# Accumulating the second third of Down's weight sums behind chunk 4's gated parts, with norm 2's vectors and one form tile moved

## The chip, the cores and the metric

The kernel runs on one core of one Trainium2 chip. The metric is device time in microseconds from the start of the program to its end; the profile describes one execution in detail, and the timed runs give the median.

## What is computed

One decoder layer on 256 tokens of width 1024: a causal pooling mixer and block attention side by side, a cross-attention into 256 memory tokens, and a gated feed-forward part of width 2816, each followed by a residual and a layer norm. The change lies in the last part.

```python
def swiglu(h, w_gate, w_up, w_down):
    return (jax.nn.silu(h @ w_gate) * (h @ w_up)) @ w_down

# per layer
h = layer_norm(ALPHA * h + mix, ln1_g, ln1_b)
h = layer_norm(ALPHA * h + memory_cross_attention(h, mem, w_xq, w_xkv, w_xo), ln2_g, ln2_b)
h = layer_norm(ALPHA * h + swiglu(h, w_gate, w_up, w_down), ln3_g, ln3_b)
```

## The kernel before

**Numbers in two parts.** Every matrix product is made from values split into a high part (rounded, by ACT, line 159 for weights) and a low part (the remainder, by DVE, line 175), with three matmuls in place of one. So each 512 KB block of weights passes through SP's load (line 107; line 104 for blocks that hold one quarter), ACT's cast and DVE's subtraction before PE can use it. `Stream` does this in order; there are seven raw places for loads, and a load is issued when DVE's subtraction has freed one. The blocks have numbers: w65 to w68 are chunk 0 of gate and up, four more for each chunk, w85 to w98 the row chunks, w99 to w102 chunk 7, w103 to w106 chunk 8, and so on.

**Feed-forward, first half.** Gate and up are computed in chunks of 256 columns, `for c in range(1, NFC)`. Chunks 5 and 6 (`ROWS`) are computed together by `Rows`, a seven-product scheme for 2 x 2 blocks that needs sums and differences of the activations (`make_forms`, in the tiles `extra0` and `extra1`) and of the weights. Every other chunk is a `Gated`: PE fills four PSUM banks (lines 482 and 488), `add` has ACT copy and DVE add their halves (lines 1331 and 1332), `multiply` applies silu and the product, and `split` makes the forms of the result and its two parts (lines 717 to 719, 534 and 535). The results of chunk c are added at the end of its turn, and multiplied and split within the turn of the next. Odd chunks use the banks of one PSUM pool, even ones those of the other, so a chunk waits for the `add` of the chunk two before; the row products start with the odd pool and come to banks of chunk 4 with their sixth product. Their own sums leave their banks through `Rows.leave` (lines 1424 to 1439), beginning with an ACT copy on line 1424; chunk 7 needs those banks.

**Feed-forward, second half.** Down uses the same seven-product scheme for nine of eleven chunks (`SUMMED`) and needs sums of weight quarters. DMA makes them in DRAM, in thirds: SP copies quarters from `w_sum` to `sum_z` and `sum_w` (`begin_sums`, line 424, and `begin_second`, line 428, tied to the loads of chunks 1, 2 and 8), and POOL adds to them with accumulating transfers (`add_quarters`, line 435): first a double quarter into `sum_z`, then, when that has landed, one of its halves into `sum_w`:

```python
def add_quarters(i):
    js = slice(i * THIRD, (i + 1) * THIRD)
    add_to(sum_z[:, :, js], w_sum[:, 2:4, js])
    add_to(sum_w[:, js], sum_z[:, 1, js])
```

The second third is read by the loads of Down's chunks 4 to 6, from w128 on.

**Order.** The schedule is written out by hand: each engine runs its instructions in the order in which the program text issues them, and `run(gu, n)` advances PE's generator by n steps between other work. POOL has little to do but these transfers and a few small norm operations, and a transfer that waits holds up all behind it on POOL.

**Norm 2.** The rows of token tile 0 are first brought to mean 0 and variance 1, which suffices for the feed-forward input; `vectors` later applies gain and bias in four DVE operations (lines 939 and 941, two each), for the residual of norm 3. They free the tile `gb2` with gain and bias.

**Places.** Tiles of 8 KB a partition share eleven places in the pool `ap` and one in the pool `late`; a new tile takes a free place. The place in `late` holds weights of chunk 0 (w67) and, from chunk 8 on, the gated parts of chunk 8.

Of the kernel before, what the change touches and what calls it, by code (L numbers as in the profile page):

```python
# [8 lines left out]
F32 = mybir.dt.float32  # L9
F32R = mybir.dt.float32r  # L10
# [4 lines left out]
P = 128  # L15
D = 1024
S = 256
T = S // P
KD = D // P
# [24 lines left out]
ROWS = (5, 6)  # L44
# [5 lines left out]
def r32(t):  # L50
    return t.bitcast(F32)


class Stream:
# [136 lines left out]
    def next(self):  # L191

        if not self.held:
            self.prepare(min(self.used + self.ahead, len(self.tiles) + 1))
# [27 lines left out]
def decoder_layer(  # L222
# [3 lines left out]
    nc = tc.nc  # L226
# [4 lines left out]
    ap = ctx.enter_context(tc.tile_pool(name="acts", bufs=A8_BUFS))  # L231
    sp = ctx.enter_context(tc.tile_pool(name="small", bufs=3))
# [6 lines left out]
    def a8(name, dt=F32):  # L239
        return ap.tile([P, KD, S], dt, tag="a8", name=name)  # L240
# [193 lines left out]
    def add_to(dst, src):  # L434
        nc.gpsimd.dma_start(dst, src, accum_op=OP.add, max_dma_last_dim=8192)  # L435
# [5 lines that stand above are left out]
# [33 lines left out]
    def proj_both(pss, numbers, yT, group=KD):  # L474

        for k0 in range(0, KD, group):
            for k in range(k0, k0 + group):
                hi, _ = ws.get(numbers, k)  # L480
                for b, ps in enumerate(pss):
                    nc.tensor.matmul(ps, hi[:, b * P:(b + 1) * P], yT.both(k), start=k == 0, stop=False,  # L482
                                     skip_group_check=True)
                yield
            for k in range(k0, k0 + group):
                _, lo = ws.parts_of(numbers, k)
                for b, ps in enumerate(pss):
                    nc.tensor.matmul(ps[:, S:], lo[:, b * P:(b + 1) * P], yT.pair(k)[0], start=False,  # L488
                                     stop=k == KD - 1, skip_group_check=True)
                ws.done(numbers, k)  # L490
                if ws.pace == 1:
                    ws.next()
                yield
# [31 lines left out]
    def run(gen, n=None):  # L525

        while n is None or n > 0:
            if next(gen, gen) is gen:
                return False
            n = None if n is None else n - 1  # L530
        return True
# [339 lines left out]
    late = ctx.enter_context(tc.tile_pool(name="late", bufs=LATE_BUFS))  # L871
# [410 lines left out]
    gT, shared = {}, []  # L1282
# [26 lines left out]
    def gated_t():  # L1309
        pt = bank("pgt").rearrange("p (f t) -> p f t", f=2)  # L1310
        for t in range(T):
            for f in range(2):
                nc.tensor.transpose(pt[:, f, t * P:(t + 1) * P], sg0[:, t, f * P:(f + 1) * P], ident)
        gated_parts(0)
        split(gT[0][0], gT[0][1], pt.rearrange("p f (t s) -> p (f t) s", t=T))
# [32 lines left out]
    def make_forms():  # L1348

        q = h2f.rearrange("p (j f) (t s) -> p j f t s", f=2, t=2)  # L1350
        at = {(f, t): q[:, :, f, t] for f in range(2) for t in range(2)}
        nc.vector.tensor_sub(at[1, 1], at[0, 1], at[1, 1])
        yield
        nc.vector.tensor_sub(at[0, 1], at[0, 0], at[0, 1])
        yield
        nc.vector.tensor_sub(at[0, 0], at[1, 1], at[0, 0])
        yield
        nc.vector.tensor_add(at[1, 0], at[1, 0], at[0, 0])
        yield
        for j in (0, 4):  # L1360
            hi, lo = (y[:, j:j + 4] for y in extra)
            nc.scalar.copy(hi, h2f[:, j:j + 4])
            yield
            nc.vector.tensor_sub(lo, h2f[:, j:j + 4], r32(hi))
            yield
# [109 lines left out]
    run(proj_n({1: first[1]}, c_gu[0], h2T))  # L1475
    gated_row(1, first[1])
    left, rows, later = None, None, norms[0].vectors()
    extra = [a8(f"extra{i}", F32R) for i in range(2)]
    more_forms = make_forms()
    for c in range(1, NFC):  # L1480
        if c == ROWS[0]:
            run(more_forms)
            rows = Rows()
            gu = rows.products()
            run(gu, 3)
            left.multiply()
            run(gu, 3)
            left.split()
            run(gu, 16)
            ws.held = True  # L1490
            run(gu)
            ws.held = False
            left = rows
        if c in ROWS:
            continue
        pss = [(accbank if c % 2 else bank)("pg") for _ in range(4)]
        if c == 3:
            ws.ahead += 1
            ws.widen("spare", sp)
            for i in range(2):  # L1500
                add_quarters(i)
        if c == 7:
            add_quarters(2)
        gu = proj_both(pss, c_gu[c], h2T, KD if c < NFC - 3 else 4)
        run(gu, 2)
        if left:
            left.multiply()
        run(gu, 2)
        if c < ROWS[0]:
            run(more_forms, 2)  # L1510
        if left and left is rows:
            run(gu, 3)
            left.transposed()
            left.split()
        elif left:
            left.split()
            run(later, 2)
        else:
            run(gu, 4)
            gated_t()  # L1520
        if c >= 2:
            run(gu, 7)
            ws.held = True
        run(gu)
        left = Gated(c, pss)
        left.add()
        ws.held = False
# [174 lines left out]
```

## Time and profile before

| what | value |
|---|---|
| median of 3 runs | 397.82 us (397.03 to 397.84) |
| profiled execution | 393.9 us |
| its span, first to last instruction | 391.6 us |
| PE busy | 367.2 us, 94% |
| DVE busy | 342.3 us, 87% |
| ACT busy | 231.8 us, 59% |
| POOL busy | 36.4 us, 9% |
| hardware DMA queue q1 | 93.41 MB, 64.7% of 16 engines |
| software DMA queue q0 | 13.37 MB, 17.2% of 16 engines |

All times in the rows below count from the start of the span. A timeline row is one instruction, or several alike in sequence, with the idle time of its engine before it and what ended that, in brackets. q0 carries the transfers that POOL issues, q1 those of SP. PE's busy time is modelled, so its idle times say more than its busy share.

### The profile page before, as it was taken

The page shows a single profiled execution, that of the slowest core. Times are in us where ns is not written, and L with a number is a line of the kernel's source. Part 1 is how long each engine was busy: PE and PEld are TensorE (multiplying, and loading weights), DVE is VectorE, ACT ScalarE, POOL GpSimd, SP SyncE. Part 2 cuts the span into 40 slices and gives each one's busy share as a digit, 9 for nine tenths or more (in the row PEclk, how much of TensorE's full clock was granted, in tenths as well). Part 3 has the DMA queues.
Part 4 walks back from the last instruction along what each step waited for, and adds up shares of the span by engine and source line. Part 5 has one row for each costly group of instructions (what it writes and reads, how often), then busy time and mean ns, then how long its engine had stood idle before and what let it go on. Part 6 is the DMA issues. An engine that isn't in the chain of part 4 may idle for free.

```text
span 391.6 us, 5502 instructions
## 1 busy us (share of the span) xinstructions
PE 367.2 (94%) x1941; PEld 311.7 (80%) x1941; DVE 342.3 (87%) x523; ACT 231.8 (59%) x356; POOL 36.4 (9%) x41
## 2 busy tenths in 40 slices
PE   9999999999999999999999999296489999999994
PEld 8888878888888899888888888284269888888882
DVE  6889899999999999899695889886767889899995
ACT  5768766774544756764474556565437756677702
POOL 0000047300310010000210000001000000000003
PEclk9999999999999999999999999689599999999999
DMA  7999996879869999999999984469997456889602
GB/s 262 412 412 362 258 402 199 330 231 338 233 142 324 386 368 261 354 315 413 270 294 256 343 271 166 154 215 347 304 344 257 157 180 200 284 284 318 230 0 107
DMA packets 33754, 107.58 MB, mean 275 GB/s; under 512 B 3264, under 2 KB 4544, under 8 KB 32320
## 3 DMA queue, kind: packets, MB, share of 16 engines
q1 hardware_dynamic: 31056, 93.41, 64.7%
q0 software_dynamic: 2240, 13.37, 17.2%
q10 hardware_dynamic: 432, 0.46, 0.3%
q8 instruction: 15, 0.25, 0.2%
q14 instruction: 11, 0.09, 0.1%
HBM read 106.18 MB, written 27.79 MB: 342 GB/s over the span
## 4 chain that ended last, share of the span: by engine, by line
PE 72%; DVE 13%; DMA 7%; issue 4%; ACT 3%; DVEq 0%; ACTq 0%
PE pg L482 11%; PE pg L488 6%; DMA w107r<-in_w_gu 5%; PE pxq L482 4%; PE pxk L482 4%; PE pqk L601 4%; PE m L467 3%; PE m L469 3%; PE m L468 3%; PE x L467 2%; PE x L469 2%; PE x L468 2%; PE pqk L604 2%; PE pxk L488 2%; PE pxq L488 2%
## 5 line engine op out<-in xcount | busy, mean ns | idle before, releaser
L534 ACT CAST g<-sq 128x1024 fp32r<-128x1024 f32 x9 | 9.4, 1050 | 25.6 <-DVE sq L719 25.6
L535 DVE TENSOR_TENSOR g<-sq,g 128x1024 fp32r<-128x1024 f32 x9 | 11.0, 1226 | 10.2 <-ACT g L534 10.2
L906 POOL TENSOR_TENSOR rs<-mv,mhalf 128x1 f32<-128x1 f32 x6 | 4.3, 723 | 146.4 <-DVE mv L904 146.4
L482 PE MATMUL pg<-h2T,w99h 128*128 128x512 f32 x8 | 4.7, 711 | 9.0 <-ACT row L1424 8.5
L666 ACT ACTIVATE pr<-pr,mx 128x128 f32<-128x128 f32 (+1 forms) x16 | 7.1, 445 | 7.7 <-DVE mx L697 7.7
L482 PEld LDWEIGHTS pg<-h2T,w99h 128*128 128x128 f32 x8 | 2.4, 309 | 11.1 <-ACT row L1424 8.9
L895 DVE BATCH_NORM_STATS2 st<-r 128x6 f32<-128x512 f32 (+1 forms) x12 | 8.1, 672 | 0.4
L435 POOL DMA_DIRECT2D sum_z<-in_w_sum x3 | 3.5, 1155 | 51.2 <-DMA sum_z<-in_w_sum 51.2
L467 PE MATMUL g<-w85h,extra 128*128 128x512 f32 x1 | 0.8, 794 | 7.4 <-DVE sq L1332 7.4
L560 ACT ACTIVATE h2f<-tp,turned 128x128 f32<-128x128 f32 x8 | 3.0, 455 | 7.0 <-PE tp L557 7.0
L911 DVE SCALAR_TENSOR_TENSOR r<-r,mv,gb 128x512 f32<-128x512 f32 (+2 forms) x10 | 6.9, 725 | 0.1
L435 POOL DMA_DIRECT2D sum_w<-sum_z x3 | 2.5, 841 | 44.1 <-DMA sum_z<-in_w_sum 44.1
L467 PEld LDWEIGHTS g<-w85h,extra 128*128 128x128 f32 x1 | 0.3, 287 | 7.8 <-DVE sq L1332 7.8
L1336 ACT ACTIVATE sq<-sq 128x512 f32<-128x512 f32 x8 | 5.1, 636 | 1.9 <-DVE sq L1332 1.9
L1012 DVE TENSOR_TENSOR r<-r,u 128x512 f32<-128x512 f32 x6 | 6.0, 1012 | 0.1
L1332 DVE TENSOR_TENSOR sq<-pg,sq 128x256 f32<-128x256 f32 x16 | 6.0, 416 | 0.0
L1332 DVE TENSOR_TENSOR sg<-pg,sg 128x256 f32<-128x256 f32 x16 | 6.0, 415 | 0.0
L809 ACT CAST xkTh<-pxk 128x256 fp32r<-128x256 f32 x8 | 2.6, 377 | 5.7 <-PE pxk L488 5.7
L922 ACT ACTIVATE h<-r,rs 128x512 f32<-128x512 f32 x2 | 1.3, 718 | 7.3 <-DVE r L911 7.3
L666 ACT ACTIVATE xpr<-xs,mx 128x256 f32<-128x256 f32 x6 | 2.8, 470 | 4.7 <-DVE mx L677 4.7
L1337 DVE TENSOR_TENSOR sq<-sq,sg 128x512 f32<-128x512 f32 x8 | 5.5, 687 | 0.1
L766 POOL TENSOR_TENSOR win<-upad 128x542 f32<-128x542 f32 x2 | 4.0, 1992 | 16.0 <-DVE upad L799 16.0
(1371 smaller groups left out, 1405.4 us busy)
## 6 DMA issues: line engine op xcount, KB each, us to landing
sum_z<-in_w_sum SPq DMA_DIRECT2D x3, 1536.0 KB, 17.9
sum_z<-in_w_sum POOLq DMA_DIRECT2D x3, 1536.0 KB, 15.2
sum_w<-in_w_sum SPq DMA_DIRECT2D x3, 768.0 KB, 14.7
sum_w<-sum_z POOLq DMA_DIRECT2D x3, 768.0 KB, 10.5
gs_z<-in_w_gs SPq DMA_DIRECT2D x1, 2048.0 KB, 9.6
gs_z<-in_w_gs POOLq DMA_DIRECT2D x1, 2048.0 KB, 18.0
wr<-in_w_qkv SPq DMA_DIRECT2D x5, 256.0 KB, 4.3
mr<-in_mem_t SPq DMA_DIRECT2D x1, 1024.0 KB, 11.5
```

The lines of the kernel that those rows point to most:

```text
L467: nc.tensor.matmul(ps, wa, ya, start=start, stop=False, skip_group_check=part)
L468: nc.tensor.matmul(ps, wa, yb, start=False, stop=False, skip_group_check=part)
L469: nc.tensor.matmul(ps, wb, ya, start=False, stop=stop, skip_group_check=part)
L482: nc.tensor.matmul(ps, hi[:, b * P:(b + 1) * P], yT.both(k), start=k == 0, stop=False, skip_group_check=True)
L488: nc.tensor.matmul(ps[:, S:], lo[:, b * P:(b + 1) * P], yT.pair(k)[0], start=False, stop=k == KD - 1, skip_group_check=True)
L534: nc.scalar.copy(h, ps)
L535: nc.vector.tensor_sub(l, ps, r32(h))
L601: nc.tensor.matmul(qk[i], part(i)[0], xT.both(k), start=first, stop=False, skip_group_check=True)
L604: nc.tensor.matmul(qk[i][:, S:], part(i)[1], x_hi, start=False, stop=last, skip_group_check=True)
L666: nc.scalar.activation(dst[:, j, :], src[:, j, :], AF.Exp, bias=mx[:, j:j + 1], scale=sign, accum_out=sm[:, j:j + 1])
L895: nc.vector.bn_stats(self.st[:, self.n, :], self.r[:, c0:c1] if src is None else src)
L1332: nc.vector.tensor_add(y[:, f, :], ps[:, :S], y[:, f, :])
```

## The change

Four edits. `extra0` is taken from `late` in place of `ap`. At chunk 3 only the first third is accumulated. The second third follows `left.split()` of chunk 4 inside the row chunks, and a small POOL copy that reads chunk 4's low part stands ahead of it, so that POOL's queue waits there for that split. The four operations of `vectors` no longer run two by two behind the splits of chunks 1 and 2, but all four behind the splits of chunks 5 and 6, in chunk 7.

```diff
     left, rows, later = None, None, norms[0].vectors()
-    extra = [a8(f"extra{i}", F32R) for i in range(2)]
+    extra = [pool.tile([P, KD, S], F32R, tag="a8", name=f"extra{i}") for i, pool in enumerate((late, ap))]
     more_forms = make_forms()
...
             run(gu, 3)
             left.split()
+            gate = sp.tile([P, 2], F32, name="sm", bufs=6)
+            nc.gpsimd.tensor_copy(gate, r32(gT[ROWS[0] - 1][1][:, 0, 0:2]))
+            add_quarters(1)
             run(gu, 16)
...
             ws.widen("spare", sp)
-            for i in range(2):
-                add_quarters(i)
+            add_quarters(0)
         if c == 7:
             add_quarters(2)
...
             left.transposed()
             left.split()
+            run(later)
         elif left:
             left.split()
-            run(later, 2)
```

## Rows read from the trace of the kernel before

**Rows 1.** The page's slices, 40 of 9.8 us each, busy tenths

```profile
PE   9999999999999999999999999296489999999994
...
PEclk9999999999999999999999999689599999999999
DMA  7999996879869999999999984469997456889602
```

**Rows 2.** The chain of waits from 200 us: start us, us, what

```profile
214.94 3.83 PE pg L488 x32
218.77 7.29 PE pg L482 x32
...
268.53 18.98 DMA w107r<-in_w_gu
...
292.08 0.92 PE pg L482 x4
```

**Rows 3.** Timeline of PE: start us, us, engine line op names shapes xcount, idle before

```profile
251.81 0.79 PE L467 MATMUL g<-w85h,extra 128*128 128x512 f32 x1 [7.38 <-DVE sq L1332]
...
279.06 0.80 PE L482 MATMUL pg<-h2T,w99h 128*128 128x512 f32 x1 [8.46 <-ACT row L1424]
...
290.59 0.30 PE L1452 MATMUL pgt<-ident,row 128*128 128x128 f32 x1 [1.24 <-DVE row L1443]
```

**Rows 4.** Timeline of DVE, 214 to 304 us

```profile
214.08 1.23 DVE L175 TENSOR_TENSOR w80l<-w80r,w80h 128x1024 fp32r<-128x1024 f32 x1 [3.80 <-ACT w80h L159]
...
222.00 0.68 DVE L939 TENSOR_TENSOR r<-r,gb 128x512 f32<-128x512 f32 x1
...
236.12 0.69 DVE L941 TENSOR_TENSOR r<-r,gb 128x512 f32<-128x512 f32 x1
...
251.34 0.75 DVE L1332 TENSOR_TENSOR sq<-pg,sq 128x256 f32<-128x256 f32 x2
...
259.65 1.23 DVE L535 TENSOR_TENSOR g<-sq,g 128x1024 fp32r<-128x1024 f32 x1 [1.12 <-ACT g L534]
...
302.49 0.75 DVE L1332 TENSOR_TENSOR sq<-pg,sq 128x256 f32<-128x256 f32 x2
```

**Rows 5.** Timeline of ACT, 213 to 279 us

```profile
213.00 1.05 ACT L159 CAST w80h<-w80r 128x1024 fp32r<-128x1024 f32 x1 [3.98 <-DMA w80r<-in_w_gu]
...
277.48 1.04 ACT L159 CAST w105h<-w105r 128x1024 fp32r<-128x1024 f32 x1 [2.05 <-DMA w105r<-in_w_gu]
278.43 0.58 ACT L1424 COPY row<-g 128x512 f32<-128x512 f32 x1
```

**Rows 6.** Timeline of POOL, its accumulating transfers

```profile
199.50 0.84 POOL L435 DMA_DIRECT2D sum_w<-sum_z  x1 [10.86 <-DMA sum_z<-in_w_sum]
200.10 1.35 POOL L435 DMA_DIRECT2D sum_z<-in_w_sum  x1
...
272.19 1.04 POOL L435 DMA_DIRECT2D sum_z<-in_w_sum  x1 [51.20 <-DMA sum_z<-in_w_sum]
```

**Rows 7.** DMA queues in 268:276, 276:287, 204:218 (two): packets, MB, share of 16 engines

```profile
q1 hardware_dynamic: 750, 3.24, 101.1%
...
q0 software_dynamic: 270, 1.57, 69.6%
...
q0 software_dynamic: 379, 2.23, 77.6%
q1 hardware_dynamic: 386, 1.41, 26.9%
```

**Rows 8.** Timeline of SP, first and last of six issues

```profile
262.04 0.33 SPq L107 DMA_DIRECT2D w102r<-in_w_gu  x1
...
266.44 0.54 SPq L107 DMA_DIRECT2D w105r<-in_w_gu  x1
```

**Rows 9.** DMA issues of the whole run: KB each, median us to landing

```profile
sum_z<-in_w_sum SPq DMA_DIRECT2D x3, 1536.0 KB, 17.9
...
w105r<-in_w_gu SPq DMA_DIRECT2D x1, 512.0 KB, 10.9
```

## The prediction

> **What bounds the kernel now.** I read the page's slices first, then the chain of waits, then the timelines of PE, DVE, ACT, POOL and SP one by one, and last the DMA view cut to three stretches. In the slices PE is full everywhere except about 244 to 291 us, where it falls twice, its granted clock falls behind each hole to one half (1.2 of 2.4 GHz), and the DMA share goes from 4 tenths to 9 in the same place [rows 1]. Everything the change touches works there or just ahead of it; from 294 us PE is full again to near the end, so a delay that PE has taken by then stays to the end. The largest single piece of the chain there is a weight load: w107r, 18.98 us from issue to landing [rows 2].
>
> The two holes in PE's timeline: 7.38 us until 251.81, waiting for DVE's L1332, and 8.46 us until 279.06, waiting for ACT's L1424; a third, 1.24 us until 290.59, waits for DVE's L1443 [rows 3]. They have different causes. In the first, the row products need a PSUM bank of chunk 4, which is free when DVE has added chunk 4's two halves (251.34); DVE is late with that because its queue is behind since 214.08, when it started w80l after a wait of 3.80 us [rows 4], which came from ACT, which had waited 3.98 us for w80r to land [rows 5]. In the second, ACT's copy L1424, which frees the bank for chunk 7, stands in ACT's queue behind the cast of w105 (277.48), and that cast starts when w105r lands [rows 5]. So the first hole is a DVE backlog with a DMA cause, the second is a DMA wait outright.
>
> **What the POOL queue's accumulations cost the loads.** Call the six accumulating transfers Z0, W0, Z1, W1, Z2, W2 (third i, the double quarter and the single one). POOL issues W0 at 199.50, Z1 at 200.10, W1 once Z1 has landed, Z2 at 272.19 [rows 6]. From 268 to 276 the hardware queue is alone and moves 3.24 MB in 8 us, 405 GB/s: so Z2's first packets come about 4 us after its issue. From 276 to 287 Z2 moves its 1.57 MB; from 204 to 218 W0 and Z1 take 77.6% of the engines, and the hardware queue moves 1.41 MB, 101 GB/s [rows 7]. While a Z is active (11 us) a 512 KB load therefore takes 5.2 us in place of 1.3. A W has half the bytes: I take 5.5 us.
>
> The Trainium skill ("DMA: Bandwidth & Descriptors", section "Queues, rings and completion order") says that each DMA engine goes round the queues that have work, a packet at a time. Read as equal shares, the hardware queue would keep some 205 GB/s beside an accumulation; the rows show half of that: the turns are equal in number, 379 packets against 386, but an accumulating packet holds its engine 2.9 times as long (77.6 to 26.9) [rows 7]. What equal shares would do to the time is a rival below.
>
> **The change part by part.**
> Z1 and W1 leave the stretch 204 to 230. W0 alone is then active from about 203.5 (199.50 + 4) to 209.0. ACT waits for w80r from 209.02 to 213.0 [rows 5]; what still moves in these 3.98 us at 101 GB/s, 0.40 MB, takes 1.0 us at 405, and with some tenths for the tail it lands near 210.3: ACT and DVE come 2.7 us forward. Bounds: 0 (the load is late for another reason) and 3.98 (the whole wait). PE is full in this stretch and gains nothing at once.
>
> Norm 2's four vector operations leave DVE's queue: two follow chunk 1's split, two chunk 2's. The first starts at 222.00, the fourth at 236.12, 0.68 and 0.69 us each; in sequence a pair takes 1.33 us [rows 4]. Both pairs stand between DVE's late start and the add at 251.34, in a stretch where DVE is without a pause but for 1.1 us at each split: 2.7 us.
>
> Together DVE reaches chunk 4's add 2.7 + 2.7 = 5.3 us (rounded) earlier, at 246.0. The first hole shrinks from 7.4 to 2.1 us; it cannot give more than 7.4. The rest of the row stage is paced by DVE's weight remainders, so PE ends it at 270.6 - 5.3 = 265.3. The clock lost after the first hole mostly comes back, but DVE sets the pace there, so I count nothing for it.
>
> The four operations go behind the splits of chunks 5 and 6 in chunk 7. There DVE's add of chunk 7 starts at 302.49 [rows 4] and is two pairs of 0.75, so it ends at 304.0, with 2.7 more at 306.7. PE wants those banks for chunk 9: the transposes end at 292.08, the rest of chunk 7 is 0.92 and 3.83, chunk 8 is 7.29 and 3.83 [rows 2], which makes 307.9. So the four fit, with about 1 us to spare. I cost them at nothing; without that cover they would cost up to the 2.7. The normed row itself is wanted only by norm 3.
>
> The form tile in the late place costs nothing: the weight tile that held it is read last in chunk 0, long before the form is written; the place it leaves is what lets chunk 4's gated parts do without the place of norm 2's gain and bias, which is now held until chunk 7. If that were wrong, chunk 4's split would wait; I see no reader that makes it. The small gate copy on POOL costs POOL under 1 us and holds up only the accumulations, which is its use.
>
> **Where Z1 and W1 go.** POOL now waits for chunk 4's split, DVE's L535 that starts at 259.65 and takes 1.23 [rows 4]. With 5.3 us off it ends at 255.6, and Z1 is issued near 256.3. On SP's queue, the next thing behind the same DVE work is w102r (262.04, so 256.7), then the copies for the last third and w103r to w105r (the last at 266.44, now 261.1) [rows 8]. Up to and with w105 that is four loads of 0.52 MB, one copy of 1.57 MB and one half that size: 4.46 MB [rows 9]. In the kernel before this stood ahead of any accumulation: w105 landed at 266.44 + 10.9 = 277.4, just when Z2 came up. Now Z1 starts with it. Step by step, in the new times: 256.7 to 258, SP still handing out, 0.3 MB; Z1 active 258 to 269, 1.1 MB at 101 GB/s; then POOL issues W1 on Z1's landing (near 269.5), and 4 us pass until its packets: to 273.5, 1.8 MB at 405 GB/s. The copy of the last third has landed near 272.7 (2.1 MB and 2 us), so Z2 is issued before W1 ends, and W1 and Z2 run without a pause, as W0 and Z1 did, from 273.5 to 290. By 273.5 there are 3.2 MB; the missing 1.26 MB at 101 GB/s take 12.5 us: 286. A load lands 2 to 4 us after that sum (before, 4.46 MB at 405 GB/s from 262.04 give 273.0, and 277.4 was measured). So w105 lands near 288; if Z1 starts 2 us later or the loads keep a little more, near 284; at the latest with Z2's end, 290.
>
> From there: cast of w105 at 288.0 in place of 277.48, PE starts chunk 7 1.58 us later, at 289.6; its 28 matmuls to the transposes took 279.06 to 289.35, 10.3 us with half the clock at first, and the clock has been idle again: 299.9. Before, the transposes began at 290.59 [rows 3], held up by w107's remainder, and had a further short wait inside; now w107 lands near 292.5, its remainder and L1443 are over by 297, so that wait is gone. Transposes end at about 300.9, not 292.1: **8.8 us later**. DVE's gain of 5.3 is inside that figure. PE is full from there on, so nothing is given back.
>
> **The sum.** Span 391.6 + 8.8 = 400.4; the profiled execution stood at 393.9, 2.3 more than its span, so 402.7 by its own measure. The median of the runs shown is 397.82, 3.9 above that execution; the same 8.8 on it gives **406.6 us**. With w105 at 284 or 290, 402.6 to 408.6.
>
> **The rivals.**
> First, faster: the accumulation fits into slack. The DMA is 4 to 6 tenths busy in the slices from 235 to 264 [rows 1]; if Z1 got through ahead of SP's copies, or the hardware queue kept its 405 GB/s beside it, w105 would come as long after its issue as before, all steps 5.3 us earlier: 392.5 us. It decides at whether w105 lands before about 277. Against it: the gate and SP's copies hang on DVE instructions 1 us apart, so Z1 cannot get ahead, and from 204 to 218 the loads fell to a quarter [rows 7]. Chance 0.14.
>
> Second, equal shares of the DMA engines: 205 GB/s for the loads. Then Z1 runs 258 to 273, 3.4 MB of loads by then and w105 complete at 275.6, landing near 277.6; PE starts chunk 7 as before and only the 1.24 us ahead of the transposes go: 396.5 us. The rows from 204 to 218 show half of that rate [rows 7]. Chance 0.06. (The round robin that the Trainium skill states in "DMA: Bandwidth & Descriptors", taken as halves, would work like this.)
>
> Third, a draw: only Z1 is ahead of w105, W1 and Z2 come up later than I think (the gap between two accumulations longer). Then 3.06 MB remain at 269 and take 7.6 us: w105 lands at 278.6 to 280, the transposes begin within 1 us of before: 397.8 us. The 4 us gap is seen before Z2 and nothing suggests that it doubles. Chance 0.07.
>
> Fourth, worse: the DVE backlog does not come from the accumulations, part of the change thus not doing what it is made for. Then only the vectors count, 2.7 in place of 5.3: 409.2 us. Chance 0.08.
>
> **How the numbers follow.** Forecast 0.65, the rivals 0.14, 0.06, 0.07, 0.08. About 0.2% (0.8 us) is what a measurement of this kernel can tell from no change. Faster takes the first two, 0.20; of the draw 0.06 lies within 0.2% and 0.01 is slower; slower is 0.74. The range goes from 396.0, which takes in the draw and the equal shares, to 410.0, which takes in the fourth case; left out are the first rival and a little above, less than 0.2 together.
>
> **What would show it.** Right: the wait for L1332 near 2 us; POOL issuing at about 256, 270, 273 and 291; w105's cast near 288; PE's wait for L1424 near 24 us in place of 8.5; w107 no longer the one that PE waits for; full PE from 301 on, and the vectors in chunk 7 with nobody waiting. Wrong: w105's cast before 280 (then Z1 cost less than its rows say), a wait for L1332 still at 5 or more (the backlog had another cause), or a new wait of PE between 301 and 350.

## The result and the profile after

The change made the kernel slower: 402.18 us median of 4 runs (401.27 to 403.68), beside 397.42 for the kernel before on the same chip (395.70 to 397.84). The ratio is 1.0132, with a 95% interval of 1.0085 to 1.0178. On another chip six runs gave 402.11 and 1.015 [1.0117, 1.0182]. Ratios in this document leave out the executions more than 1.5% above the fastest of their kernel, while medians and ranges are of all, so a ratio can differ a little from the quotient of two medians. The profiled execution took 401.27 us with a span of 399.4; before it was 393.9 and 391.6, so the spans differ by 7.8 us. That is 3.0 more than the medians do (4.8): the traced run of before was a short one for its kernel, and the split of the 7.8 us below is one of two traced runs.

The page's slices of after (40 of 10.0 us each, busy tenths) answer to [rows 1]:

```profile
PE   9999999999999999999999998940589999999992
...
PEclk9999999999999999999999999985599999999998
DMA  7999997779769999999997554699995555889602
```

The first hole (slice 25, 240 to 250 us) has nearly closed; the second is much deeper, with one slice of no PE work at all, and the granted clock falls to half (1.2 of 2.4 GHz) once instead of twice between 240 and 300 us. PE's waits from 190 to 310 us, as engine, line waited for, us in total, times, longest:

```profile
PE pg L482 <- ACT row L1424: 19.8, 1, 19.8
PE g L467 <- DVE sq L1332: 1.5, 1, 1.5
PE pgt L1452 <- DVE row L1443: 1.5, 2, 1.3
```

They answer to the three idle times in [rows 3]: 7.38 became 1.5, 8.46 became 19.8, and 1.24 stayed at 1.3. The timeline of ACT (start us, duration, what, idle before and what ended it) shows where the first two come from:

```profile
209.65 1.05 ACT L159 CAST w80h<-w80r 128x1024 fp32r<-128x1024 f32 x1 [0.50 <-DMA w80r<-in_w_gu]
...
281.98 1.04 ACT L159 CAST w105h<-w105r 128x1024 fp32r<-128x1024 f32 x1 [4.83 <-DMA w105r<-in_w_gu]
282.93 0.58 ACT L1424 COPY row<-g 128x512 f32<-128x512 f32 x1
...
292.39 1.05 ACT L159 CAST w107h<-w107r 128x1024 fp32r<-128x1024 f32 x1 [3.92 <-DMA w107r<-in_w_gu]
```

Against [rows 5], w80's cast starts 3.4 us earlier and has nearly no wait left; w105's starts 4.5 us later, and the copy L1424 that frees PE's bank stands right behind it. POOL's timeline says what moved, and answers to [rows 6]:

```profile
256.00 1.07 POOL L435 DMA_DIRECT2D sum_z<-in_w_sum  x1
273.80 0.84 POOL L435 DMA_DIRECT2D sum_w<-sum_z  x1 [16.73 <-DMA sum_z<-in_w_sum]
274.39 1.31 POOL L435 DMA_DIRECT2D sum_z<-in_w_sum  x1
293.56 0.85 POOL L435 DMA_DIRECT2D sum_w<-sum_z  x1 [17.85 <-DMA sum_z<-in_w_sum]
```

These are Z1, W1, Z2 and W2. The DMA view cut to the stretches 258 to 269, 270 to 277 and 278 to 292 us (packets, MB, share of 16 engines) answers to [rows 7]:

```profile
q0 software_dynamic: 244, 1.49, 70.3%
q1 hardware_dynamic: 259, 1.39, 32.4%
...
q1 hardware_dynamic: 658, 2.67, 97.7%
...
q0 software_dynamic: 379, 2.23, 77.5%
q1 hardware_dynamic: 378, 1.37, 26.2%
```

The three stretches are Z1 beside the loads, the loads alone, and W1 with Z2 beside the loads. The hardware queue moves 126, 381 and 98 GB/s. Before, the loads from w102 to w105 had the engines to themselves until Z2 came. On SP's queue w105r was issued at 260.99, 5.4 us earlier than in [rows 8], and landed 20.9 us later, beside 10.9 in [rows 9].

Last, the chain of waits of after from 262 us (start us, us, what), against [rows 2]:

```profile
262.53 29.84 DMA w107r<-in_w_gu
...
295.95 0.98 PE pgt L1452 x7
296.94 0.92 PE pg L482 x4
...
312.83 3.67 PE pg L482 x16
316.52 1.22 DVE w113l L175
317.74 0.69 DVE w114l L175
...
371.48 6.36 DMA w150r<-in_w_down
```

The transposes end at 296.94, 4.86 us later than in [rows 2]. From there to the end of the span it takes 399.4 - 296.94 = 102.5 us, where before it took 391.6 - 292.08 = 99.5. So the 7.8 us are 4.9 lost by the transposes and 2.9 lost behind them, and the second part has a sign in the chain: from 316.52 on it runs over DVE's weight remainders, where before it stayed on PE to about 349. The page's share of PE in the chain fell from 72% to 51%, that of DVE rose from 13% to 22%.

### The profile page after: what moved, and what is told of

It reads as the page before. It is cut to its first block, busy times and chain, and to the rows that moved or that the text cites. A ratio compares the mean times of both kernels' runs of the same rounds, so it can differ in the third digit from the quotient of the medians.

```text
span 399.4 us, 5504 instructions
## 1 busy us (share of the span) xinstructions
PE 365.7 (92%) x1941; PEld 309.2 (77%) x1941; DVE 342.2 (86%) x523; ACT 231.3 (58%) x356; POOL 37.4 (9%) x42
## 4 chain that ended last, share of the span: by engine, by line
PE 51%; DVE 22%; DMA 12%; issue 8%; ACT 5%; ACTq 0%; DVEq 0%
DMA w107r<-in_w_gu 7%; PE pxq L482 4%; PE pxk L482 4%; PE pqk L601 3%; PE pg L482 3%; DMA w80r<-in_w_gu 2%; PE x L467 2%; PE x L468 2%; PE x L469 2%; PE pg L488 2%; PE pxk L488 2%; PE pxq L488 2%; PE pu L482 2%; PE xv L467 2%; PE pqk L604 2%
## 5 line engine op out<-in xcount | busy, mean ns | idle before, releaser
L534 ACT CAST g<-sq 128x1024 fp32r<-128x1024 f32 x9 | 9.4, 1049 | 24.9 <-DVE sq L719 24.9
L482 PE MATMUL pg<-h2T,w99h 128*128 128x512 f32 x8 | 4.7, 711 | 20.3 <-ACT row L1424 19.8
L175 DVE TENSOR_TENSOR w103l<-w103r,w103h 128x1024 fp32r<-128x1024 f32 x1 | 1.2, 1224 | 11.1 <-ACT w103h L159 11.1
L159 ACT CAST w103h<-w103r 128x1024 fp32r<-128x1024 f32 x1 | 1.0, 1044 | 12.3 <-DMA w103r<-in_w_gu 12.3
L1490 POOL COPY sm<-g 128x2 f32<-128x2 f32 x1 | 1.1, 1116 | 55.5 <-DVE g L535 55.5
L1332 DVE TENSOR_TENSOR sq<-pg,sq 128x256 f32<-128x256 f32 x16 | 6.0, 417 | 0.0
L1332 DVE TENSOR_TENSOR sg<-pg,sg 128x256 f32<-128x256 f32 x16 | 6.0, 417 | 0.0
## 6 DMA issues: line engine op xcount, KB each, us to landing
mr<-in_mem_t SPq DMA_DIRECT2D x1, 1024.0 KB, 11.7
```

The lines of the kernel that those rows point to most:

```text
L534: nc.scalar.copy(h, ps)
L1332: nc.vector.tensor_add(y[:, f, :], ps[:, :S], y[:, f, :])
```

## The experiments

Two theories stood at the start. Theory A: the loss is Z1 and W1 lying on the loads of w103 to w105, which ACT's copy L1424 has to wait for; the gain is a DVE backlog that shrinks. Theory B: the loss comes from the vectors in their late place. "Tail" below is the time from the end of the transposes to the end of the span, in the profiled execution.

**1. Only the accumulations moved.** The kernel before, with the gate and Z1, W1 behind chunk 4's gated parts:

```diff
             left.split()
+            gate = sp.tile([P, 2], F32, name="sm", bufs=6)
+            nc.gpsimd.tensor_copy(gate, r32(gT[ROWS[0] - 1][1][:, 0, 0:2]))
+            add_quarters(1)
...
-            for i in range(2):
-                add_quarters(i)
+            add_quarters(0)
```

> Only the accumulation of the second third moves behind chunk 4's split; norm 2's vectors and the form tile stay as in the kernel before. Theory A (the two accumulations collide with the loads of w103 to w105, and that alone makes PE late): DVE reaches chunk 4's add about 3.3 us earlier than before, near 248, w105's cast starts near 284 to 285, PE's wait for L1424 is near 19 us, the transposes of chunk 7 begin about 7 us later than before, and the time is about 7 us over before, within 1 us of the changed kernel. Theory B (the loss comes from the vectors in chunk 7): the time is at or under that of before.

Measured: 403.29 us (402.12 to 404.23), ratio 1.0192 [1.012, 1.0264]. PE's waits:

```profile
PE pg L482 <- ACT row L1424: 20.9, 1, 20.9
PE g L467 <- DVE sq L1332: 5.1, 1, 5.1
```

This part alone gives the whole loss. w80's cast comes at 210.76, 2.2 us earlier than before, and 2.3 us of the first hole go with the accumulations. w105's cast comes at 286.89. The transposes end at 300.41 and the tail is 99.9 us, with the chain on PE to about 357: none of the late loss is there. Theory B is out as the main cause.

**2. Only the vectors moved.** After, without the gate, and with `for i in range(2): add_quarters(i)` back at chunk 3.

> Only norm 2's vectors (with the form tile's place) move; both thirds are accumulated at chunk 3 as before. Theory A: the first hole of PE shrinks from 7.4 to 4.7 us, everything up to chunk 7's transposes comes 2.7 us earlier, and then DVE, 2.7 us behind from 303 on, gives it back by the end: within 1 us of before. Theory B: the vectors in chunk 7 cost the 5 to 7 us of the changed kernel here too. If the forecast's zero price for them were right: 2.7 us under before.

Measured: 395.82 us (393.09 to 400.64), ratio 0.9994 [0.9955, 1.0034]: no change. The first hole is 4.4 us in place of 7.4, but the second is 10.5 in place of 8.5: w105r is issued 1.1 us earlier than before (265.32), but Z2 1.8 us earlier (270.39), Z2's packets reach the engines from 274 on, before w105 is in, and w105's cast is at 278.14. The transposes end 0.5 us earlier than before, and the tail is 102.6. So the vectors give on one side of the transposes and take on the other. The two sides do not add up to the equal medians: the traced run here is 2.6 us longer than the traced run of before, which was a short one, and with one trace of each the balance is not shown more closely.

**3. The vectors in PE's hole.** After, with all four vectors ahead of w103's remainder, where DVE waits for the load:

```diff
-            run(gu, 16)
+            run(gu, 11)
+            run(later)
+            run(gu, 5)
...
-            run(later)
```

> The changed kernel, but the four vector operations stand in DVE's queue ahead of w103's remainder, where DVE waits 11.1 us for that load. Theory A, with the vectors costing at the end what they save in front: 2.5 us under the changed kernel, the chain after 316 us on PE again, not on DVE. If DVE's lateness at the end has another cause (the later loads): no difference from the changed kernel.

Measured: 400.62 us (399.33 to 401.58), ratio 1.0117 [1.0028, 1.0207], 1.6 us under the median of after, which was measured on another chip; 2.5 was expected. The tail is 100.5 us and the chain stays on PE, so the 2 us of the tail came back. What took part of them is at the transposes:

```profile
297.25 1.76 PE pgt L1452 x7
299.01 1.71 PE pg L482 x4
```

In after the same pieces take 0.98 and 0.92 us. PE had waited 1.9 us for L1443 just ahead of them, against 1.3 in after. Its granted clock, full (1.00) from 291 to 297, was at half (0.50) from 297.5 to 300.5; in after it stays full. The other runs of this kernel were not traced; two of them took 399.33 and 399.87 us, the traced one 401.37.

**4. The accumulations elsewhere.** Experiment 3, with the gate on chunk 2's gated parts instead of chunk 4's:

```diff
             left.split()
-            gate = sp.tile([P, 2], F32, name="sm", bufs=6)
-            nc.gpsimd.tensor_copy(gate, r32(gT[ROWS[0] - 1][1][:, 0, 0:2]))
-            add_quarters(1)
...
         elif left:
             left.split()
+            if c == 3:
+                gate = sp.tile([P, 2], F32, name="sm", bufs=6)
+                nc.gpsimd.tensor_copy(gate, r32(gT[c - 1][1][:, 0, 0:2]))
+                add_quarters(1)
```

> As e3, but the second third is accumulated behind chunk 2's split, near 231 us, where the DMA engines have slack until 256. Theory A: DVE as early as in the changed kernel (chunk 4's add near 245.4), the loads w88 to w98 slowed but not late, w105's cast near 271.5, PE's wait for L1424 back at about 8.5 us, and 6 us under before, some 391 us. Rival: the loads of the row chunks come too late and the first hole opens again, to 5 us or more; then at or over before.

Measured: 388.89 us (388.58 to 389.17), ratio 0.9829 [0.9765, 0.9894], faster than before: the interval lies below 1. Its transfers and waits, first POOL's timeline, then PE's waits:

```profile
232.13 1.07 POOL L435 DMA_DIRECT2D sum_z<-in_w_sum  x1
246.31 0.84 POOL L435 DMA_DIRECT2D sum_w<-sum_z  x1 [13.11 <-DMA sum_z<-in_w_sum]
267.25 1.04 POOL L435 DMA_DIRECT2D sum_z<-in_w_sum  x1 [20.10 <-DMA sum_z<-in_w_sum]
```

```profile
PE pg L482 <- ACT row L1424: 11.0, 1, 11.0
PE g L467 <- DVE sq L1332: 2.3, 1, 2.3
```

The same two transfers, 24 us earlier, cost PE nothing that its waits show: the first hole (2.3) is that of experiment 3 (2.5), and w105's cast is at 273.94. The transposes end at 287.01, 5.1 us earlier than before. This is the gain of the change without its loss.

**5. After again**, on the chip of 6 to 8. 

> The changed kernel once more, on the chip of e6 to e8, to compare them with. 1.2 to 2% over before.

Measured: 402.11 us (401.84 to 402.97), ratio 1.015 [1.0117, 1.0182]; span 400.0, waits 20.6 (L1424) and 1.8 (L1332), transposes' end 297.37, tail 102.6, DVE's chain from 316.95 on.

**6. After without the vectors** (`run(later)` left out, so token tile 0 lacks norm 2's gain and bias).

> The changed kernel without norm 2's gain and bias for token tile 0 (this part of the computation is left out). Theory A (from 316 us on the changed kernel is bound by DVE, which the four vectors in chunk 7 have put behind): 2.0 to 2.7 us under e5, and the chain after 300 runs over PE until about 357. If the vectors are hidden, as forecast: the same as e5 within 0.5 us.

Measured: 400.38 us (398.76 to 401.31), ratio 1.0097 [1.006, 1.0134], 1.7 us under experiment 5. The tail is 100.2 us against 102.6, and the chain is on PE to 390; so the vectors cost 2.4 us behind the transposes. Ahead of them the traced run loses 1.8 us, much as experiment 3 did: PE waited 2.1 us for L1443, the transposes ran at half clock (1.76 us for the seven) and ended at 299.17. The spans thus differ by 0.6 alone. The edit cannot be the cause of that loss, since the vectors stand behind the transposes; the traced run is the longest of its six.

**7. After without Z1 and W1** (the gate and `add_quarters(1)` left out, so the second third's sums are not made).

> The changed kernel without the accumulation of the second third (Z1 and W1 left out; Down's chunks 4 to 6 then use unsummed quarters). Theory A (Z1 and W1 in that place cost the whole delay of w105): w105's cast near 272 to 274, PE's wait for L1424 near 10 us in place of 19.8, transposes of chunk 7 near 286, and about 10 us under e5, some 392. Rival (the third third's own copies and Z2 set w105, and Z1 only takes their place): under 3 us less than e5.

Measured: 391.77 us (390.65 to 391.88), ratio 0.9877 [0.9831, 0.9922], 10.3 us under experiment 5. PE's waits:

```profile
PE pg L482 <- ACT row L1424: 10.8, 1, 10.8
PE g L467 <- DVE sq L1332: 1.9, 1, 1.9
```

w105's cast is at 273.91, 9.5 us before that of experiment 5 and the same as in experiment 4, where Z1 and W1 run behind chunk 2. The price of the two transfers is therefore 10 us in the one place and none that the traces show in the other. The tail is 102.5 us: the vectors' price is there with or without the accumulations.

**8. The last third's copies later.** What is left of the second hole in experiments 4 and 7, 11 us, should be the 2.36 MB of the last third's copies on SP's queue ahead of w103. So the kernel before, with them tied to chunk 10's loads:

```diff
-    for i, c in enumerate((1, 2, 8)):
+    for i, c in enumerate((1, 2, 10)):
```

> The kernel before, with only the copies for the last third tied to chunk 10's loads in place of chunk 8's; Z2, which waits for them, comes later too. Theory A (w103 to w105 are late in the kernel before because 2.36 MB of copies and then Z2 stand ahead of or beside them): w105's cast near 268 in place of 277.5, PE's wait for L1424 under 3 us in place of 8.5, and 6 to 9 us under before, some 389. Rival (the stretch is bound by DVE, which is busy with weight remainders in any case): under 3 us less.

Measured: 396.77 us (394.51 to 398.89), ratio 1.0025 [0.9994, 1.0056]. W2 went out ahead of the copy that it adds to, so that copy overwrites what W2 added, and SP stood from 277.7 to 303.8 us until the copy could go. The second hole shrank to 3.5, but a new one of 4.4 us opened behind it, for loads that stood behind SP's wait. Nothing follows from this time; experiment 9 mends the order.

**9. The same, with the last third's additions one chunk later too.**

```diff
-    for i, c in enumerate((1, 2, 8)):
+    for i, c in enumerate((1, 2, 10)):
...
-        if c == 7:
+        if c == 8:
             add_quarters(2)
```

> The kernel before with the last third's copies tied to chunk 10's loads and its additions issued in chunk 8, behind both copies (in e8 the additions to the single quarter were issued ahead of its copy). Theory A: w103 to w105 no longer wait behind 2.36 MB of copies, w105's cast near 273 to 275 (DVE and ACT are as late as before by then), PE's wait for L1424 near 3.5 us in place of 8.5, and 3 to 6 us under before. Rival (DVE bounds the stretch anyhow, or the copies now delay w111 to w115 as much): under 1 us less.

Measured: 387.63 us (385.88 to 389.05), ratio 0.9783 [0.9714, 0.9851]. PE's waits:

```profile
PE g L467 <- DVE sq L1332: 9.1, 2, 7.8
PE pg L482 <- ACT row L1424: 3.6, 1, 3.6
```

The first hole is close to that of before (7.8 to 7.4), as it must be; the second fell from 8.5 to 3.6 us. w105r is issued at 268.27, later than in [rows 8], and its cast waits 0.36 us. Z2 comes later too (284.65), and no run moves the copies without it. Its share is the smaller one: in experiment 4 its packets lay beside the loads only from 271 on, and the 0.47 MB that the loads moved from there to 274 take 1.2 us at 405 GB/s, so Z2 can have cost w105 about 2 us (an estimate), where experiment 10 has w105's cast 7.4 us earlier than experiment 4.

**10. Experiments 4 and 9 together.** 

> e4 and e9 together: second third behind chunk 2's split, last third with chunk 10's loads, vectors ahead of w103's remainder. Theory A: DVE 6 us earlier at chunk 4's add, w105's cast near 267, PE's waits for L1332 and L1424 near 2 and 3 us: 3 to 6 us under e4, some 384 to 386. Against it: with w103 early, the vectors no longer stand in a gap of DVE and cost up to 2.7 us.

Measured: 384.06 us (383.11 to 385.31), ratio 0.9696 [0.9634, 0.9759]: faster than both kernels. PE's waits:

```profile
PE pg L482 <- ACT row L1424: 3.8, 1, 3.8
PE pg L482 <- DVE row L1426: 3.5, 1, 3.5
PE g L467 <- DVE sq L1332: 1.7, 1, 1.7
```

The gap in DVE's queue that hid the vectors in experiments 3 and 4 is gone here: they run from 265.29 to 268.03, and L1426, which PE waits for, comes behind them.

**11. Experiment 10 with the vectors behind the splits of chunks 1 and 2, as before.** 

> As e10, but the vectors two by two behind the splits of chunks 1 and 2, as in the kernel before. If they cost nothing where e10 has them: 1 to 2.7 us over e10. If e10 has no gap left for them: the same within 1 us.

Measured: 384.53 us (383.78 to 384.70), ratio 0.97 [0.9629, 0.9771]. The wait for L1426 goes to 0.9 and that for L1332 back to 4.8: with both holes short, the vectors cost about the same in either place.

The runs side by side (holes by PE's longest wait for each line; end of the transposes and tail from the chain of waits and the span):

| kernel | median us | hole L1332 | hole L1424 | w105's cast | transposes end | tail |
|---|---|---|---|---|---|---|
| before | 397.42 | 7.4 | 8.5 | 277.48 | 292.08 | 99.5 |
| after | 402.18 | 1.5 | 19.8 | 281.98 | 296.94 | 102.5 |
| 1 accumulations alone | 403.29 | 5.1 | 20.9 | 286.89 | 300.41 | 99.9 |
| 2 vectors alone | 395.82 | 4.4 | 10.5 | 278.14 | 291.56 | 102.6 |
| 3 vectors in the hole | 400.62 | 2.5 | 20.1 | 283.25 | 299.01 | 100.5 |
| 4 gate at chunk 2 | 388.89 | 2.3 | 11.0 | 273.94 | 287.01 | 99.8 |
| 5 after again | 402.11 | 1.8 | 20.6 | 283.40 | 297.37 | 102.6 |
| 6 no vectors | 400.38 | 2.3 | 19.7 | 283.43 | 299.17 | 100.2 |
| 7 no Z1, W1 | 391.77 | 1.9 | 10.8 | 273.91 | 287.21 | 102.5 |
| 9 last third late | 387.63 | 7.8 | 3.6 | 273.78 | 286.57 | 99.7 |
| 10 4 and 9 | 384.06 | 1.7 | 3.8 | 266.56 | 281.42 | 99.8 |
| 11 10, vectors early | 384.53 | 4.8 | 3.6 | 269.47 | 282.72 | 100.2 |

## Why the prediction came out as it did

The time fell inside the range, on the forecast side, by the mechanism named, but that it came as near as it did is in part luck. Of the 4.4 us between 406.6 and 402.18, 1.0 is in the span (400.4 forecast, 399.4), 0.4 in what lies around it (2.3 taken, 1.9), and 3.0 in the carry to the median: I put 3.9 on the profiled execution because before's median stood that far above it, and after's stands 0.9 above. Before's own executions spread from 392.66 to 399.94 us on one chip, while experiment 4's lie within 0.6; why is open. The profile of before was simply one of its shorter runs.

The 1.0 in the span is small because two errors of it nearly cancel: the second hole was forecast too long, and the tail too short. Step by step:

- **The load of w80 comes earlier, 2.7 us.** Right, 3.4. Experiment 1, where the accumulations alone moved, has 2.2. The wait in [rows 5] was, for the most part, the accumulations' cost: 0.5 us of it is left.
- **DVE reaches chunk 4's add 5.3 us earlier, at 246.0; the first hole falls to 2.1.** Right: the timeline of DVE has it at 245.34, and the hole is 1.5. Experiments 1 and 2 have the two halves: holes of 5.1 and 4.4 us.

```profile
245.34 0.75 DVE L1332 TENSOR_TENSOR sq<-pg,sq 128x256 f32<-128x256 f32 x2
...
253.66 1.23 DVE L535 TENSOR_TENSOR g<-sq,g 128x1024 fp32r<-128x1024 f32 x1 [1.11 <-ACT g L534]
...
294.62 1.28 DVE L1443 TENSOR_TENSOR row<-row,row 128x512 f32<-128x512 f32 x2
```

- **The clock lost after the first hole counts for nothing.** Nearly right: the granted clock, at half from 248 to 258 before, stays full, and PE is through the row stage at 263.8 in place of 265.3; 0.8 us of that is a shorter stage (18.0 us from its first product, 18.8 before).
- **Z1 is issued near 256.3, active from 258.** Right: 256.00, with packets from 258.
- **The loads beside an accumulation get 101 GB/s.** Mis-sized for Z1: 126 (1.39 MB in 11 us), and right for W1 and Z2: 98. That is 0.3 MB more, or 0.7 us of loads alone. The packets were near equal in number beside Z1 too (259 to 244), but those of the hardware queue, where the last third's copy stood ahead of w103, carried 5.4 KB each (1.39 MB in 259) and those beside W1 and Z2 3.6 (1.37 in 378).
- **W1 is issued at 269.5 and has packets from 273.5.** This is the step that failed. Z1's packets were as good as done by 270, but the last ten of them were spread to 274 between the loads' packets; Z1 landed for POOL at 273.80, and W1's packets came 4 us behind that, just ahead of 278. So the loads had the engines alone for 7 to 8 us in place of the 4.5 that I gave them, and moved 2.67 MB in place of 1.8. With 0.3 before 258, 1.39 beside Z1 and 2.67 alone, 4.4 of the 4.46 MB were through by 277. I took the pause before Z2 in [rows 6, 7] for that between two accumulations that depend on one another; the pause before W1 has a second part, the landing of Z1. The trace of before shows little of that part: the last packets of Z1 with any bytes lie between 218 and 219 us, POOL has the landing at 220.15, and W1's packets come from 224, some 5 us in which that queue moves next to nothing, where after has 7 to 8. Why Z1's last packets took so long in after is not shown.
- **w105's cast near 288, PE's wait for L1424 near 24 us.** 281.98 and 19.8: both follow from the step before, the wait being longer by the 1.5 us that PE came early. They stand between the forecast and the third rival (278.6 to 280), whose mechanism, a longer gap between the accumulations, was half there. Experiment 7 puts the cost of Z1 and W1 in that place at 10.3 us outright.
- **w107 is no longer what PE waits for ahead of the transposes.** Wrong: it landed when forecast (292.4 for 292.5), but PE was there nearly 6 us earlier than forecast (294.2 for 299.9), and L1443 at 294.62 still held it for 1.3. The transposes ended 4.9 us later than before, not 8.8.
- **The vectors cost nothing in chunk 7, PE is full from 301 on, nothing is given back.** Wrong by 2.9 us in the tail. I looked at one need alone, PE's for chunk 9's banks, and the fit of "about 1 us to spare" at one place. There it holds: PE has one new wait behind the transposes, 0.8 us for L1332 at 338.66. But the vectors' 2.7 us stay in DVE's queue to the last loads. From the transposes to w143's remainder DVE waits the same 6.7 us in after as before, all of it for ACT (L534 and w121's cast), so there is no slack that could take up the delay. That remainder, behind which the load w150r goes out, starts 73.8 us after the transposes in all four kernels with vectors in chunk 7 (after, 2, 5, 7), and 71.1 to 71.5 in the eight without (before, 1, 3, 4, 6, 9, 10, 11). In before the load stands 2.7 us nearer to the transposes' end than in after:

```profile
363.88 6.53 DMA w150r<-in_w_down
```

  The tail was 102.5 to 102.6 us in the four and 99.5 to 100.5 in the eight (experiment 8 has a hole of its own there and is left out). The bound that I gave, "up to the 2.7", was the right number, and I took nothing in its place.
- **The form tile and the gate copy cost nothing.** No wait in the trace of after names the gate copy, and experiment 4, which has both, is 7.6 us under before (388.89, 396.46 on the same chip). Neither was run by itself.

Two rivals fell with numbers. Equal shares: 379 packets against 378 moved 2.23 and 1.37 MB, the time shared 77.5 to 26.2. (The round robin by packets of the Trainium skill, "DMA: Bandwidth & Descriptors", section "Queues, rings and completion order", agrees with these counts; to read it as halves of the bandwidth was the error of that rival.) Slack: Z1 behind chunk 4 does not fit, since the same two transfers behind chunk 2 are 11.7 us cheaper (experiments 3 and 4). The fourth rival, that the first hole had another cause, is refuted by experiments 1 and 2: w80's cast is at 210.76 where the accumulations alone moved, and at 214.17 where they stayed.

What remains open: whether moving Z1 by less than two chunks would do as well (behind chunk 3 wasn't tried), what Z1's late landing comes from, and how the last third's copies and Z2 share the rest of the second hole.

## What to carry to other kernels

A transfer that is taken out of one crowded stretch has to be put where the loads beside it have nobody waiting: list the loads that will be in flight with it, and the first in-order instruction behind each. Here the deciding one was a copy that had nothing to do with the load, and stood behind its cast in ACT's queue. A vector operation moved into a later stage is free only if its engine has slack at some point from there to the end; check the engine's whole remaining queue, not the next deadline. Here DVE had none, and the 2.7 us of the vectors went through to the last load.

## What the runs showed of the hardware

- While an accumulation runs beside loads, its packets and theirs are equal in number (379 and 378 in after, 379 and 386 before), and an accumulating packet holds its engine three times as long (77.5% of the engines' time to 26.2%) for 5.9 KB in place of 3.6 (2.23 and 1.37 MB). The loads fall from 381 GB/s to 98.
- From the issue on POOL to the first packets it took 3 to 4 us where the hardware queue filled the engines (272.19 to 276 before, 273.80 to 278 in after, 246.31 to 249 in experiment 4), and 2 us where it did not (256.00 to 258 in after, 232.13 to 234 in experiment 4).
- A transfer whose packets are all but done can land 4 us late: eight of Z1's packets fell in 270 to 272 us and two in 272 to 274, between 358 of the loads'.
- In experiments 3 and 6 PE's granted clock had come back to full by 291 us after the hole of 20 us, and fell to half again at the transposes, where PE had waited 1.9 and 2.1 us just ahead of them; in after and experiment 5, where it had waited 1.3 us and 0.2, it stayed full. The seven transposes took 1.76 us at half clock and 0.98 at full.
